# Background products of an attention stage in another order, their weights split half a block ahead, and the heads' loads issued by SP

## The chip, the cores and the metric

The kernel runs on one core of a Trainium2 chip. The metric is the device time of one execution in microseconds (us), taken as the median of several runs. The core's engines each work through a list of instructions of their own, in a fixed order: TensorE (PE) multiplies matrices and writes to the banks of PSUM, VectorE (DVE) and ScalarE (ACT) work element by element, GpSimd (POOL) helps, and SyncE (SP) only issues transfers (DMAs). They wait for each other by semaphores.

## The reference

One decoder layer for a sequence of 512 positions of 1024 channels, in fp32, one layer deep:

```python
x = x + 0.5 * swiglu(rms_norm(x, ffn1_norm), ffn1_w_gate, ffn1_w_up, ffn1_w_down)
h = rms_norm(x, mix_norm)
z = h @ w_in      # its columns: c_q | c_kv | k_rope | dq | dk | dv | gate_mla | gate_diff
y_mla  = mla_branch(c_q, c_kv, k_rope, ...)      # 8 heads, low-rank q and kv, causal
y_diff = diff_branch(dq, dk, dv, ...)            # 4 heads, softmax1 - lambda * softmax2, causal
merged = (sigmoid(gate_mla) * (y_mla @ w_proj_mla)
          + sigmoid(gate_diff) * (y_diff @ w_proj_diff))
x = x + merged @ w_out
x = x + 0.5 * swiglu(rms_norm(x, ffn2_norm), ffn2_w_gate, ffn2_w_up, ffn2_w_down)
return rms_norm(x, final_norm)
```

## The kernel before

Activations lie transposed, channels on the 128 partitions and the 512 positions along the rows. Every fp32 operand is split into a high part rounded to fp32r (names that end in h or hi) and the rest (l or lo), and a product is three matmuls in a row: high weights times low, and so on (`mm3`, lines 116 to 119). A block of weights comes by a DMA on SP's queue into one of two halves of the buffer `raw` (`load`, line 102). `split` (lines 109 and 110) lets ACT cast it to `whi` and DVE subtract that from it to give `wlo`; for seven of the blocks it is POOL that subtracts.

This case is about the middle of the program, the two attention branches. Their own matmuls are short and each step has to pass through a softmax on DVE and ACT, so other matmuls are put between the steps. These are the products of the normed input with the columns of `w_in` for the gates and for dq and dk of the second branch. A product of 128 columns has eight steps (k = 0 to 7) of three matmuls each. The products are written as Python generators, chained into `stream`; `fill(n)` advances it by n steps, and it is called after each attention step as often as `MLA_FILL` and `DIFF_FILL` say. At its first step a product loads its weights, splits them, and multiplies.

- `make_gates(nm, n2)`: two products from one load of 256 columns. Behind each, DVE scales the bank (line 822, `gate`), ACT takes the tanh, and the result is stored to DRAM (`gm_d` or `gd_d`).
- `diff_qk(h)`: the products dq and dk of head h. Behind each, the rotary work: ACT copies the bank to `zr`, SP sends four small DMAs that swap rows (`sw`, lines 843 and 844), DVE makes `z` in three instructions (lines 846 to 848), ACT casts it (`zh`), DVE subtracts (`zl`), and the parts are stored to `qad`, `kad` and `kld` in DRAM.
- The first branch (MLA) takes eight heads of four steps: scores (`bank_sc<-kth,...`), softmax, transposes (`bank_tp<-ident,e`, `ptl`), values (`bank_pv`). Six jobs run beside it, and what is left of them runs behind it.
- The second branch (diff) takes four heads. `diff_load(h)` brings a head from DRAM: `qa`, `ka`, `kl` in two halves, and `dv`, on ACT's queue. A step of `diff_scores` makes two scores of up to 512 columns (lines 992 and 993), each followed by softmax_block: DVE adds the mask and takes the extremum (line 807), ACT takes the exponential (line 809). Then DVE combines both (lines 999 to 1001), PE transposes (line 1009), ACT and DVE split the result into `pt0` and `pt1` (lines 1010 and 1011), and a step later PE multiplies with `dv` (line 1019), and DVE adds the halves (line 1023).

PSUM banks go by tags: three for scores (`sc`), two for the background products (`gb`), two for transposes (`tp`), one for values (`pv`). A fourth score waits until the exponential of the first has read its bank.

The order on each engine in this part isn't that of the code alone: the framework's scheduler decides it when the program is built. On the chip it is then fixed.

Of the kernel before, what the change touches and what calls it, by code (L numbers as in the profile page):

```python
# [15 lines left out]
P = 128  # L16
# [3 lines left out]
KT = DM // P  # L20
# [36 lines left out]
def hybrid_layer_kernel(ctx: ExitStack, tc: tile.TileContext, x, positions,  # L57
# [6 lines left out]
    nc = tc.nc  # L64
# [34 lines left out]
    def load(view, eng=None):  # L99
        _, a, b = view.shape  # L100
        t = space(a, b)
        (eng or nc.sync).dma_start(out=t, in_=view)
        return t
# [708 lines left out]

    def make_gates(nm, n2):
        raw = load(kview(w_in, off[nm] + n2 * 256, off[nm] + (n2 + 1) * 256))
        for s in range(2):
            yield
            ps = bank()

            eng = pool if nm == "gm" and (n2 or s) else vec
            yield from gemm_steps(ps, split(raw[:, :, s * P:(s + 1) * P], eng), kcols, xg)  # L820
            g = zp.tile([P, T], F32, name="gate", tag="z")
            vec.tensor_tensor(out=g, in0=ps, in1=Rb, op=ALU.mult)
            act.activation(g, g, AF.Tanh, scale=0.5)
            nc.sync.dma_start(out=gd_[nm][n2 * 2 + s], in_=g)

# [7 lines left out]
    def diff_qk(h):  # L833
        for j, nm in enumerate(("dq", "dk")):
            yield
            raw = load(kview(w_in, off[nm] + h * P, off[nm] + (h + 1) * P))
            ps = bank()
            yield from gemm_steps(ps, split(raw), kcols, xg)
# [23 lines left out]
        spilled.add(h)  # L862


    jobs = [diff_qk(0), make_gates("gm", 0), diff_qk(1), make_gates("gm", 1), make_gates("gm", 2), make_gates("gm", 3)]
    stream = (u for job in jobs for u in job)
# [98 lines left out]
    jobs = [diff_qk(2), make_gates("gd", 0), diff_qk(3), make_gates("gd", 1), make_gates("gd", 2), make_gates("gd", 3)]  # L965
    stream = (u for job in jobs for u in job)
    heads = {}

    def diff_load(h):
# [7 lines left out]
        act.dma_start(out=as_f32(qa), in_=qad[h].rearrange("(s a) r t -> (a r) s t", s=2))  # L977
        act.dma_start(out=as_f32(ka), in_=kad[h].rearrange("(s a) r t -> (a r) s t", s=2))
        for s in range(2):
            rs = slice(64 * s, 64 * s + 64)  # L980
            act.dma_start(out=as_f32(kl[rs, s, :]), in_=kld[h, rs, :])
        act.dma_start(out=as_f32(dv), in_=dvd[:, h].rearrange("p b u c -> p b (u c)"))
# [66 lines left out]
    diff_load(0)  # L1049
    steps = [(h, i) for h in range(DH) for i in range(NB)]  # L1050
# [248 lines left out]
```

## Time and profile before

| What | us |
|---|---|
| median of 3 runs | 1076.73 |
| lowest, highest run | 1076.37, 1077.65 |
| the profiled execution's own time | 1076.4 |
| its span, first to last instruction | 1074.7 |
| first branch, from its first score | about 430 to 523 |
| second branch, until its last transposes | about 523 to 632 |

The profile is of one execution. Its busy times are of each engine; matmuls are pipelined, so that one begins before the one ahead has ended, and so are DVE's instructions. The granted clock of TensorE was 0.999 of full over the span.

### The profile page before, as it was taken

Reading aid. Unit: us, or ns where it says so; the run is one execution under the profiler, and the core shown is the slowest. Engines: PE = TensorE matmul, PEld = TensorE weight load, DVE = VectorE, ACT = ScalarE, POOL = GpSimd, SP = SyncE. Lnnn points to the kernel's source line nnn. Section 1 sums busy time; section 2 is a strip of 40 time slices with the busy share of each in tenths; the row PEclk is TensorE's granted clock in tenths of the full one; section 3 lists DMA queues with packets and bytes.
Section 4 is the critical chain, followed back from the end, with each engine's and each line's share of the span. In section 5 each row is a group of like instructions: output and inputs, shape, how many; then the busy total and the mean of one; then the engine's idle time right before and its main releaser. Section 6 shows DMA issues by size and latency. Waiting matters only on the chain.

```text
span 1074.7 us, 15826 instructions
## 1 busy us (share of the span) xinstructions
PE 1058.4 (98%) x6272; PEld 934.5 (87%) x6272; DVE 811.7 (76%) x1336; ACT 513.3 (48%) x832; POOL 47.4 (4%) x57
## 2 busy tenths in 40 slices
PE   8999999999999999999999999999999999999997
PEld 6798989999898888788788888888989999898995
DVE  5998797978766767998488868558977767767753
ACT  6462534435254434676356634344525435252544
POOL 1000000000000100012100000000000000000003
PEclk9999999999999999999999999999999999999999
DMA  8314262434215415352767468321242503224211
GB/s 249 126 37 148 79 203 92 114 103 173 83 59 162 124 50 156 92 162 71 225 188 232 121 216 287 114 79 42 79 153 80 158 32 131 74 84 153 79 60 78
DMA packets 106297, 132.90 MB, mean 124 GB/s; under 512 B 4230, under 2 KB 86320, under 8 KB 106224
## 3 DMA queue, kind: packets, MB, share of 16 engines
q1 hardware_dynamic: 96448, 110.80, 32.3%
q10 hardware_dynamic: 7728, 15.18, 4.5%
q0 software_dynamic: 2048, 5.92, 2.0%
q8 instruction: 49, 0.80, 0.3%
q14 instruction: 24, 0.20, 0.1%
HBM read 114.32 MB, written 17.04 MB: 122 GB/s over the span
## 4 chain that ended last, share of the span: by engine, by line
PE 89%; DVE 5%; DMA 3%; ACT 1%; issue 1%; SPq 0%; DVEq 0%; ACTq 0%
PE bank_gb L117 8%; PE bank_gb L119 8%; PE bank_gb L118 8%; PE bank_sc L404 4%; PE bank_sc L402 4%; PE bank_sc L403 4%; PE bank_gb L402 3%; PE bank_gb L404 3%; PE bank_gb L403 3%; PE bank_tp L404 3%; PE bank_tp L403 3%; PE bank_tp L402 3%; PE bank_sc L118 3%; PE bank_sc L119 3%; PE bank_sc L117 2%; PE bank_tp L118 2%
## 5 line engine op out<-in xcount | busy, mean ns | idle before, releaser
L109 ACT CAST whi<-raw 128x1024 fp32r<-128x1024 f32 (+1 forms) x124 | 123.2, 995 | 122.6 <-PE bank_gb L119 31.2
L110 DVE TENSOR_TENSOR wlo<-raw,whi 128x1024 fp32r<-128x1024 f32 (+1 forms) x117 | 134.6, 1150 | 49.2 <-ACT whi L109 49.0
L110 DVE TENSOR_TENSOR wlo<-fraw,whi 128x1024 fp32r<-128x1024 f32 x77 | 92.1, 1196 | 43.5 <-ACT whi L109 43.5
L109 ACT CAST whi<-fraw 128x1024 fp32r<-128x1024 f32 x77 | 79.1, 1027 | 78.0 <-PE bank_gb L119 27.2
L117 PE MATMUL bank_gb<-xh,wlo 128*128 128x512 f32 x256 | 103.2, 403 | 0.5 <-DVE wlo L110 0.5
L119 PE MATMUL bank_gb<-xl,whi 128*128 128x512 f32 x256 | 100.5, 393 | 0.0
L118 PE MATMUL bank_gb<-xh,whi 128*128 128x512 f32 x256 | 100.2, 392 | 0.0
L109 ACT CAST whi<-s 128x1024 fp32r<-128x1024 f32 x36 | 37.8, 1049 | 81.4 <-PE bank_sc L119 15.2
L404 PE MATMUL bank_sc<-xl,whi 128*128 128x256 f32 x224 | 63.5, 283 | 0.0
L403 PE MATMUL bank_sc<-xh,whi 128*128 128x256 f32 x224 | 63.5, 283 | 0.0
L402 PE MATMUL bank_sc<-xh,wlo 128*128 128x256 f32 x224 | 63.5, 283 | 0.0
L119 PEld LDWEIGHTS bank_gb<-xl,whi 128*128 128x128 f32 x256 | 48.1, 188 | 10.2
L117 PEld LDWEIGHTS bank_gb<-xh,wlo 128*128 128x128 f32 x256 | 48.2, 188 | 9.1 <-DVE wlo L110 0.9
L110 DVE TENSOR_TENSOR wlo<-s,whi 128x1024 fp32r<-128x1024 f32 x36 | 44.0, 1222 | 15.8 <-ACT whi L109 15.2
L118 PEld LDWEIGHTS bank_gb<-xh,whi 128*128 128x128 f32 x256 | 48.3, 189 | 8.1
L402 PEld LDWEIGHTS bank_sc<-xh,wlo 128*128 128x128 f32 x224 | 43.0, 192 | 0.1
L403 PEld LDWEIGHTS bank_sc<-xh,whi 128*128 128x128 f32 x224 | 43.0, 192 | 0.1
L404 PEld LDWEIGHTS bank_sc<-xl,whi 128*128 128x128 f32 x224 | 43.0, 192 | 0.0
L404 PE MATMUL bank_tp<-xl,whi 128*128 128x256 f32 x144 | 40.8, 283 | 0.0
L403 PE MATMUL bank_gb<-xh,whi 128*128 128x256 f32 x144 | 40.8, 283 | 0.0
L404 PE MATMUL bank_gb<-xl,whi 128*128 128x256 f32 x144 | 40.8, 283 | 0.0
L403 PE MATMUL bank_tp<-xh,whi 128*128 128x256 f32 x144 | 40.8, 283 | 0.0
(582 smaller groups left out, 3245.8 us busy)
## 6 DMA issues: line engine op xcount, KB each, us to landing
fraw<-in_ffn_w_gate_dram SPq DMA_DIRECT2D x11, 1024.0 KB
fraw<-in_ffn_w_up_dram SPq DMA_DIRECT2D x11, 1024.0 KB
raw<-in_w_in_dram SPq DMA_DIRECT2D x11, 1024.0 KB
raw<-in_ffn_w_gate_dram SPq DMA_DIRECT2D x10, 1024.0 KB
raw<-in_ffn_w_up_dram SPq DMA_DIRECT2D x10, 1024.0 KB
fraw<-in_ffn_w_down_dram SPq DMA_DIRECT2D x4, 2048.0 KB
raw<-in_ffn_w_down_dram SPq DMA_DIRECT2D x4, 2048.0 KB
raw<-in_w_in_dram SPq DMA_DIRECT2D x8, 512.0 KB
```

The source lines that it names most:

```text
L109: act.copy(hi, src)
L110: (eng or vec).tensor_tensor(out=lo, in0=src, in1=as_f32(hi), op=ALU.subtract)
L117: pe.matmul(ps, wl, xh, start=start, stop=False)
L118: pe.matmul(ps, wh, xh, start=False, stop=False)
L119: pe.matmul(ps, wh, xl, start=False, stop=stop)
L402: pe.matmul(o, wl[:, g, k, :], th[:, k, :], start=first and n, stop=False, skip_group_check=True)
L403: pe.matmul(o, wh[:, g, k, :], th[:, k, :], start=False, stop=False, skip_group_check=True)
L404: pe.matmul(o, wh[:, g, k, :], tl[:, k, :], start=False, stop=last, skip_group_check=True)
```

## The change

The generators are taken apart into pairs of functions: `parts` loads and splits a product's weights, `product` multiplies and finishes. A new generator `units` runs them: after the fifth of a product's eight steps (k == KT // 2) it calls `parts` of the next product, so that load and split stand in the program three steps ahead of their first use. The order of jobs beside the first branch was diff_qk(0), gm 0, diff_qk(1), gm 1, gm 2, gm 3, and becomes gm 0, diff_qk(0), gm 1, gm 2, diff_qk(1), gm 3. Beside the second branch it was diff_qk(2), gd 0, diff_qk(3), gd 1, gd 2, gd 3, and becomes diff_qk(2), diff_qk(3), gd 0, gd 1, gd 2, gd 3. Eight steps (`fill(KT)`) run between the load of the first head and its first score. The five DMAs of `diff_load` move from ACT's queue to SP's.

```diff
         return e
 
 
+
     def make_gates(nm, n2):
-        raw = load(kview(w_in, off[nm] + n2 * 256, off[nm] + (n2 + 1) * 256))
-        for s in range(2):
-            yield
+        raw = []
+
+        def parts(s):
+            if s == 0:
+                raw.append(load(kview(w_in, off[nm] + n2 * 256, off[nm] + (n2 + 1) * 256)))
+
+            eng = pool if nm == "gm" and (n2 or s) else vec
+            return split(raw[0][:, :, s * P:(s + 1) * P], eng)
+
+        def product(s, w):
             ps = bank()
-
-            eng = pool if nm == "gm" and (n2 or s) else vec
-            yield from gemm_steps(ps, split(raw[:, :, s * P:(s + 1) * P], eng), kcols, xg)
+            yield from gemm_steps(ps, w, kcols, xg)
             g = zp.tile([P, T], F32, name="gate", tag="z")
             vec.tensor_tensor(out=g, in0=ps, in1=Rb, op=ALU.mult)
             act.activation(g, g, AF.Tanh, scale=0.5)
             nc.sync.dma_start(out=gd_[nm][n2 * 2 + s], in_=g)
 
+        return [(partial(parts, s), partial(product, s)) for s in range(2)]
+
 
     sws = [zp.tile([P, T], F32, name=f"sw{j}", bufs=1) for j in range(2)]
     for t in sws:
...
     spilled = set()
 
     def diff_qk(h):
-        for j, nm in enumerate(("dq", "dk")):
-            yield
-            raw = load(kview(w_in, off[nm] + h * P, off[nm] + (h + 1) * P))
+        def parts(nm):
+            return split(load(kview(w_in, off[nm] + h * P, off[nm] + (h + 1) * P)))
+
+        def product(nm, j, w):
             ps = bank()
-            yield from gemm_steps(ps, split(raw), kcols, xg)
+            yield from gemm_steps(ps, w, kcols, xg)
             zr = zp.tile([P, T], F32, name="zr", bufs=1)
             act.copy(zr, ps)
             sw = sws[j]
...
                 for u in range(4):
                     nc.sync.dma_start(out=kad[h, u], in_=hi[u // 2])
                 nc.sync.dma_start(out=kld[h], in_=as_f32(zl))
-        spilled.add(h)
-
-
-    jobs = [diff_qk(0), make_gates("gm", 0), diff_qk(1), make_gates("gm", 1), make_gates("gm", 2), make_gates("gm", 3)]
-    stream = (u for job in jobs for u in job)
+            if j:
+                spilled.add(h)
+
+        return [(partial(parts, nm), partial(product, nm, j)) for j, nm in enumerate(("dq", "dk"))]
+
+    def units(jobs, w=None):
+        us = [u for job in jobs for u in job]
+        w = w or us[0][0]()
+        for n, (_, product) in enumerate(us):
+            yield
+            for k, _ in enumerate(product(w)):
+                if k == KT // 2 and n + 1 < len(us):
+                    w = us[n + 1][0]()
+                yield
+
+
+    jobs = [make_gates("gm", 0), diff_qk(0), make_gates("gm", 1), make_gates("gm", 2), diff_qk(1), make_gates("gm", 3)]
+    stream = units(jobs)
 
     def fill(n=1):
         for _ in range(n):
...
     for t in kls:
         for s in range(2):
             pool.memset(as_f32(t[64 - 64 * s:128 - 64 * s, s, :]), 0.0)
-    jobs = [diff_qk(2), make_gates("gd", 0), diff_qk(3), make_gates("gd", 1), make_gates("gd", 2), make_gates("gd", 3)]
-    stream = (u for job in jobs for u in job)
+    jobs = [diff_qk(2), diff_qk(3), make_gates("gd", 0), make_gates("gd", 1), make_gates("gd", 2), make_gates("gd", 3)]
+    stream = units(jobs, jobs[0][0][0]())
     heads = {}
 
     def diff_load(h):
...
         ka = df.tile([P, 2, T], F32R, name="ka")
         kl = kls[h % 2]
         dv = df.tile([P, NB, 2 * P], F32R, name="dv")
-        act.dma_start(out=as_f32(qa), in_=qad[h].rearrange("(s a) r t -> (a r) s t", s=2))
-        act.dma_start(out=as_f32(ka), in_=kad[h].rearrange("(s a) r t -> (a r) s t", s=2))
+        nc.sync.dma_start(out=as_f32(qa), in_=qad[h].rearrange("(s a) r t -> (a r) s t", s=2))
+        nc.sync.dma_start(out=as_f32(ka), in_=kad[h].rearrange("(s a) r t -> (a r) s t", s=2))
         for s in range(2):
             rs = slice(64 * s, 64 * s + 64)
-            act.dma_start(out=as_f32(kl[rs, s, :]), in_=kld[h, rs, :])
-        act.dma_start(out=as_f32(dv), in_=dvd[:, h].rearrange("p b u c -> p b (u c)"))
+            nc.sync.dma_start(out=as_f32(kl[rs, s, :]), in_=kld[h, rs, :])
+        nc.sync.dma_start(out=as_f32(dv), in_=dvd[:, h].rearrange("p b u c -> p b (u c)"))
         heads[h] = qa, ka, kl, dv, df.tile([P, NB, P], F32, name="o4"), small.tile([P, 8, NB], F32, name="hst", bufs=2)
 
     def diff_scores(h, i):
...
         yd.append((yh, yl))
 
     diff_load(0)
+    fill(KT)
     steps = [(h, i) for h in range(DH) for i in range(NB)]
     pend = {}
     for k in range(len(steps) + 7):
```

The rows that follow are the orders on the engines as the program is built; a name's number tells which buffer it is. First PE in the second branch, before, where head 1 ends and head 2 begins: L1019 multiplies with `dv`, L992 and L993 are a score, L117 to L119 are steps of a background product.

```order
L1019 MATMUL bank_pv_5780<-dv_5309,pt0_5668 128x256
L1019 MATMUL bank_pv_5780<-dv_5309,pt1_5669 128x256
L992 MATMUL bank_sc_5789<-ka_5564,qa_5563 128x128
L993 MATMUL bank_sc_5789<-kl0_5261,qa_5563 128x128
L117 MATMUL bank_gb_5737<-xh1_3237,wlo_5739 128x512
L118 MATMUL bank_gb_5737<-xh1_3237,whi_5738 128x512
L119 MATMUL bank_gb_5737<-xl1_3238,whi_5738 128x512
L117 MATMUL bank_gb_5818<-xh0_3235,wlo_5820 128x512
L118 MATMUL bank_gb_5818<-xh0_3235,whi_5819 128x512
L119 MATMUL bank_gb_5818<-xl0_3236,whi_5819 128x512
```

A score of head 2 is followed by six matmuls of background products. The same place with the change, L1042 being the values, L1015 and L1016 a score:

```order
L1042 MATMUL bank_pv_5833<-dv_5356,pt0_5735 128x256
L1042 MATMUL bank_pv_5833<-dv_5356,pt1_5736 128x256
L1015 MATMUL bank_sc_5842<-ka_5627,qa_5626 128x128
L1016 MATMUL bank_sc_5842<-kl0_5261,qa_5626 128x128
L1015 MATMUL bank_sc_5859<-ka_5627,qa_5626 128x128
L1016 MATMUL bank_sc_5859<-kl0_5261,qa_5626 128x128
L1015 MATMUL bank_sc_5904<-ka_5627,qa_5626 128x256
L1016 MATMUL bank_sc_5904<-kl0_5261,qa_5626 128x256
L1042 MATMUL bank_pv_5883<-dv_5356,pt0_5825 128x256
L1042 MATMUL bank_pv_5883<-dv_5356,pt1_5826 128x256
```

Three scores of head 2 now follow each other with nothing of the background between, then values. After two more scores (bank_sc_5924, bank_sc_5975) and a transposition come 48 matmuls of gd 1 in one piece. A like run stands one head earlier (scores from bank_sc_5480 to bank_sc_5712), ahead of 48 matmuls of dk of head 3 and of gd 0.

DVE at the second of these runs, with the change (L808 is the mask with the extremum and its read-out, L1024 the combination, L111 the split):

```order
L808 ISA bank_sc_5859,hst_5635<-bank_sc_5859,cmask_3521 128x128
L808 ISA hst_5635 128x1
L1046 TENSOR_TENSOR o4_5362<-bank_pv_5883,o4_5362 128x128
L808 ISA bank_sc_5904,hst_5635<-bank_sc_5904,cmask_3521 128x256
L808 ISA hst_5635 128x1
L1022 RECIPROCAL hst_5635<-hst_5635 128x1
L808 ISA bank_sc_5924,hst_5635<-bank_sc_5924,cmask_3521 128x256
L808 ISA hst_5635 128x1
L1023 TENSOR_SCALAR hst_5635<-hst_5635,nlam_3913 128x1
L808 ISA bank_sc_5975,hst_5635<-bank_sc_5975,cmask_3521 128x384
L808 ISA hst_5635 128x1
L111 TENSOR_TENSOR wlo_5723<-raw_75,whi_5722 128x1024
```

The last row is the low part of the weights with which the 48 matmuls begin (`wlo_5723`); it stands behind the mask of the run's last score.

SP with the change, ahead of the weights of dk of head 3 (the first `raw` row) and of gd 0 (the second):

```order
L1004 DMA kl1_5262<-kld_3547 64x512
L866 DMA qad_3545<-zh_5328 64x512 x2
L867 DMA qad_3545<-zl_5329 128x512
L1004 DMA kl1_5262<-kld_3547 64x512
L1005 DMA dv_5356<-dvd_3550 128x1024
L853 DMA sw1_4119<-zr_5396 8x512
L854 DMA sw1_4119<-zr_5396 8x512
L853 DMA sw1_4119<-zr_5396 8x512
L854 DMA sw1_4119<-zr_5396 8x512
L103 DMA raw_75<-in_w_in_dram 128x8x128
L103 DMA raw_75<-in_w_in_dram 128x8x256
```

Head 1's loads stand between the stores of head 2's q (`qad`) and the four swaps of its k, and the two loads of weights behind them. Before, SP had only the stores, the swaps and the weights.

## Rows read from the trace of the kernel before

**Rows 1.** The page: the span, and part 1 (busy time and share).

```profile
span 1074.7 us, 15826 instructions
...
PE 1058.4 (98%) x6272; PEld 934.5 (87%) x6272; DVE 811.7 (76%) x1336; ACT 513.3 (48%) x832; POOL 47.4 (4%) x57
```

**Rows 2.** Busy time of each engine in the two attention stretches.

```profile
430.00:523.00 93.00, 91.39 (x482) 76.84 (x481) 82.97 (x213) 60.95 (x143) 16.79 (x7) 1.00 0.39 111
523.00:632.00 109.00, 106.97 (x550) 89.31 (x549) 85.25 (x276) 60.10 (x168) 2.09 (x4) 1.00 0.63 191
```

**Rows 3.** Waits of PE in both stretches: total us, times, longest.

```profile
PE bank_sc L993 <- DMA kl<-kld: 0.9, 1, 0.9
PE bank_sc L992 <- ACT e L809: 0.8, 2, 0.7
PE bank_pv L925 <- DVE ptl L912: 0.6, 2, 0.3
PE bank_gb L117 <- DVE wlo L110: 0.5, 1, 0.5
```

**Rows 4.** Timeline of PE at 445 us: start, length, line, names, idle before.

```profile
444.30 0.28 PE L925 MATMUL bank_pv<-ptl,vt 128*128 128x256 f32 x1
444.42 0.22 PE L924 MATMUL bank_pv<-pth,vt 128*128 128x128 f32 x1
444.47 0.28 PE L925 MATMUL bank_pv<-ptl,vt 128*128 128x128 f32 x1
445.29 0.50 PE L117 MATMUL bank_gb<-xh,wlo 128*128 128x512 f32 x1 [0.54 <-DVE wlo L110]
```

**Rows 5.** Timeline of PE and ACT at 546 us.

```profile
546.09 0.71 ACT L809 ACTIVATE e<-bank_sc,hst 128x512 f32<-128x512 f32 x1
...
546.94 0.33 PE L992 MATMUL bank_sc<-ka,qa 128*128 128x128 f32 x1 [0.67 <-ACT e L809]
...
547.51 0.39 PE L118 MATMUL bank_gb<-xh,whi 128*128 128x512 f32 x1
...
547.74 0.40 PE L119 MATMUL bank_gb<-xl,whi 128*128 128x512 f32 x1
```

**Rows 6.** Timeline of DVE at 446 us.

```profile
446.10 0.67 DVE L846 TENSOR_TENSOR z<-bank_gb,table 128x512 f32<-128x512 f32 x1
446.70 0.68 DVE L807 CUSTOM_DVE_ANT_0 bank_sc<-bank_sc,cmask 128x512 f32<-128x512 f32 x1
```

**Rows 7.** DVE by line and shape, 536 to 632 us (busy, mean ns | idle before).

```profile
L110 DVE TENSOR_TENSOR wlo<-raw,whi 128x1024 fp32r<-128x1024 f32 x10 | 12.2, 1218 | 1.6 <-ACT whi L109 1.6
L807 DVE CUSTOM_DVE_ANT_0 bank_sc<-bank_sc,cmask 128x512 f32<-128x512 f32 x8 | 5.6, 697 | 1.0 <-PE bank_sc L993 1.0
L822 DVE TENSOR_TENSOR gate<-bank_gb,Rb 128x512 f32<-128x512 f32 x8 | 5.5, 686 | 1.0 <-PE bank_gb L119 1.0
L1023 DVE TENSOR_TENSOR o<-bank_pv,o 128x128 f32<-128x128 f32 x16 | 4.5, 284 | 0.4 <-ACT o L1022 0.4
L807 DVE CUSTOM_DVE_ANT_0 bank_sc<-bank_sc,cmask 128x384 f32<-128x384 f32 x8 | 4.5, 563 | 4.8 <-PE bank_sc L993 4.8
L1000 DVE TENSOR_SCALAR hst<-hst,nlam 128x1 f32<-128x1 f32 x16 | 4.3, 270 | 0.2
...
L807 DVE CUSTOM_DVE_ANT_0 bank_sc<-bank_sc,cmask 128x256 f32<-128x256 f32 x7 | 2.9, 434 | 1.6 <-PE bank_sc L993 1.1 <-ACT e L809 0.5
...
L999 DVE RECIPROCAL hst<-hst 128x1 f32<-128x1 f32 x16 | 2.5, 159 | 1.8 <-ACT e L809 1.6
```

**Rows 8.** Timelines of SP and ACT: a weight load's issue, its landing.

```profile
556.50 0.38 SPq L102 DMA_DIRECT2D raw<-in_w_in_dram  x1
...
564.68 1.05 ACT L109 CAST whi<-raw 128x1024 fp32r<-128x1024 f32 x1 [2.30 <-DMA raw<-in_w_in_dram]
```

**Rows 9.** Timelines of POOL and DVE at 483 us.

```profile
483.18 2.40 POOL L110 TENSOR_TENSOR wlo<-raw,whi 128x1024 fp32r<-128x1024 f32 x1 [7.47 <-ACT whi L109]
...
483.72 2.41 DVE L933 TENSOR_TENSOR yml<-yf,ymh 128x512 fp32r<-128x512 f32 x1
```

More of the change, by code (lines that the diff above doesn't have):

```diff
@@ L1 @@
 import math
+from functools import partial
 from contextlib import ExitStack
```

## The prediction

> **What bounds the kernel now.** I read the page first, to see which engine has no slack. TensorE is busy for 1058.4 of 1074.7 us [rows 1], so nothing but its pauses can be won, and anything that makes it pause is lost. The table by stretch comes next: the change touches the two attention branches alone, and there TensorE is idle for 1.61 of 93 us and for 2.03 of 109 us, 3.64 together, while DVE is busy for 82.97 and 85.25 [rows 2]. The reader is to see two things there: little can be won, and DVE, which feeds both the softmax and the weight splits, is at 89% and 78% of its time, near enough to full that the order of its work matters.
>
> The waits of TensorE say what the idle time is for [rows 3]: 0.9 us for a head's `kl`, 0.8 in two waits for an exponential that frees a score bank, 0.6 in two for `ptl`, 0.5 for a split. They come to 2.8 us in six waits. A wait costs more than its idle time, because matmuls overlap: one of 512 columns lasts 0.39 us, and the next starts 0.23 after it [rows 5], so each break also takes about 0.16. From start to start the break at 445 us is 0.82 (444.47 to 445.29), where an undisturbed step is some 0.1 [rows 4]. So the six waits are worth 2.8 + 6 x 0.16 = 3.8 us. The other 0.84 of the 3.64 lies in shorter breaks.
>
> **The change part by part.** *What no sum needs.* TensorE gets the same matmuls, POOL the same seven splits, ACT loses twenty issues of transfers. Only order and waits count.
>
> *First branch.* In the new order a gate product stands first, and the two rotary pairs are farther apart. On DVE the work per head becomes more even, and a split stands three steps (nine matmuls, 9 x 0.23 = 2.1 us) ahead of its first use. The waits for `wlo` and `ptl` (1.1 us in three, 1.6 with their breaks) should go, the first wait of the softmax should stay.
>
> *Second branch, what goes.* Eight steps, 24 matmuls or 24 x 0.23 = 5.5 us, come between the load of the first head and its score, and cover the 0.9 us for `kl`. The two score waits at 546 us stand at a place that is filled otherwise now. Together 1.7 us in three, 2.2 with breaks.
>
> From both branches that is 3.8. I add the shorter breaks, 0.84, since most stand at rotary work or at transposes that move too, and get 4.6 given back. The bounds: 3.0, if a third of it comes back elsewhere, and 5.9, if the whole 3.64 goes with some fourteen breaks (14 x 0.16 = 2.2).
>
> *Second branch, what comes.* This is the heart of it. With both rotary pairs first, the fills of `DIFF_FILL` no longer spread over all heads as they did. The scheduler leaves two runs of scores, transposes and values with no product between them, and each ends before 48 matmuls that need a split. In DVE's list that split stands behind all the softmax work of the run (the rows of the order shown above). So TensorE has only the run's own matmuls to do, while DVE has to get through all that stands ahead of the split, and DVE's part is longer.
>
> The second run, as the example. I count from the transposes just ahead of its first score, for DVE can't begin the first instruction of its list (the `pt1` of those transposes) before them. From there to the split DVE has 22 instructions, besides the short read-outs, which start together with the next: seven of 512 columns (two masks, `sw`, `z`, `zl`, the gate, one combination) at about 0.69, two of 384 at 0.56, three of 256 at 0.43, five of 128 at 0.284, two `hst` at 0.27, two reciprocals at 0.16, and the split at 1.22 [rows 7]. Instructions that aren't masks are put at the row of the same width. That is 4.83 + 1.13 + 1.30 + 1.42 + 0.54 + 0.32 + 1.22 = 10.76. An instruction starts some 0.08 before the last has ended (446.10 + 0.67 against 446.70 [rows 6]); 21 x 0.08 = 1.7, so 9.1 us. To this come 0.6 until DVE can begin (the tail of the transposes and ACT's pass over 256 columns, about half of the 0.71 in [rows 5]) and 0.1 until TensorE starts again: 9.8. TensorE has meanwhile 7 matmuls of 512 columns at 0.23, 2 of 384 at 0.18 (between the two neighbours), 16 of 256 and 11 of 128 at 0.12 [rows 4, 5]: 1.61 + 0.36 + 1.92 + 1.32 = 5.2. It stands for 4.6 us.
>
> The first run in the same way: seven of 512, one of 384, two of 256, five of 128, two `hst`, four reciprocals and the like, the split: 4.83 + 0.56 + 0.87 + 1.42 + 0.54 + 0.64 + 1.22 = 10.08, less 1.7, and 0.7 at the ends: 9.1. TensorE has 7, 4, 24 and 11: 1.61 + 0.72 + 2.88 + 1.32 = 6.5. It stands for 2.6 us.
>
> Both are floors, because they let DVE run without a gap. In the trace it stands for 1.6 us ahead of seven masks of 256 columns (0.2 each) and for 4.8 ahead of eight of 384 (0.6 each) [rows 7]. I take one hand-over of 0.3 a run, between these two: 2.9 + 4.9 = 7.8. The bounds: 7.2 with none, 8.4 with 0.6 each.
>
> *The loads on SP.* The five of a head stand ahead of the weights of the next products. A weight load of 1 MB issued at 556.50 was waited for by ACT until 564.68, 8.2 us [rows 8]; the loads of the products in question are issued with some 1 to 2.6 us more than that in hand. I put them at 0. With the cover gone, each us of lateness is one us of wait at the same split: 2 to 3 us at most for the bytes of one head ahead of it.
>
> The sum: 1076.4 (the profiled execution's own time, 0.3 below the median shown) - 4.6 + 7.8 = 1079.6 us.
>
> **The rivals.**
>
> *(a) Faster: the runs are cheap.* The nearest wait that the trace shows where scores follow each other is 0.67 us, 0.83 with its break [rows 5]. Were the runs to cost this each, the sum would be 1076.4 - 4.6 + 1.7 = 1073.5. The point that decides: DVE has to have finished the split within TensorE's 5.2 and 6.5 us. For it speaks that the kernel has had only short waits at such places; against it, that the split then stood beside products that TensorE could do meanwhile.
>
> *(b) No change: floors and the whole give-back.* DVE's runs at 7.2 and 5.9 given back: 1076.4 + 1.3 = 1077.7, and up to 0.7 less if breaks too short for the idle time to show go as well. For it: each count above is of one list and its order is fixed; against it: every short break has to vanish.
>
> *(c) Slower still: transfers.* The head's loads and the weights share the way, and the weights land 2 to 3 us after the cover: 1079.6 + 2.5 = 1082.1. For it speak the 8.2 us of [rows 8], against it that SP issues long before. The Trainium skill, page "DMA: Bandwidth & Descriptors", section "Issuing engines are not separate DMA queues", says that transfers started by different engines run on the same 16 DMA engines and interleave, and that a second issuer saves only the issuing. By that rule the move from ACT to SP would win nothing at the transfers themselves. No row here shows the two issuers beside each other.
>
> *(d) Slower still: POOL beside DVE.* A split on POOL that took from 483.18 for 2.40 us had beside it a subtraction on DVE of 2.41 us that is otherwise some 0.69 [rows 9, 7]. In the first branch POOL's splits meet other DVE work now; one more such meeting on the path costs 2.41 - 0.69 = 1.7: 1081.3. Against it: there are as many such splits as before. The Trainium skill, page "SBUF — State Buffer", section "Who interferes with whom", says that a DVE instruction with two inputs in SBUF contends with a GpSimd instruction that reads SBUF, and that one fully blocks while the other has the shared ports. The row agrees, with 2.41 us.
>
> **How the numbers follow.** Some 0.2% (2.15 us, so 1074.6 and 1078.9) is what a measurement of this kernel can tell from no change. The forecast has 0.42, with 1078.9 to 1080.9 as its own range (give-back 5.3 to 3.9 against 7.8, or the runs at their ends); (b) 0.28, since its terms are only the bounds of mine; (c) 0.14; (d) 0.08; (a) 0.08. Slower: 0.42 + 0.14 + 0.08 = 0.64. No change: 0.28 and a trace of (a), 0.29. Faster: the rest, 0.07. The range reaches down to the end of (b), 1077.0, and up through (d) and most of (c), to 1082.6; (a) and the edges are left out.
>
> **What would show it.** Right: in the changed profile TensorE has two waits for `wlo` on DVE in the second branch, of about 3 and 5 us, each right ahead of 48 matmuls, and DVE is busy without a gap before them; the first branch is idle for under 0.7 us. Wrong: several short waits for score banks in place of two long ones (then DVE isn't late at the split but at the masks, and the sum may stay), a split that waits for ACT's cast and that for `raw` (rival c), or first-branch waits of the old size (the evenness was no gain). The prediction fails in size if DVE has done part of the list before the transposes from which I count.

## The result

The changed kernel takes 1083.18 us (median of 6 runs, 1082.35 to 1085.68), the kernel before, run beside it, 1077.14 (6 runs). The ratio is 1.0065, with a 95% interval of 1.0052 to 1.0078: slower by 5.6 to 8.4 us. The forecast was 1079.6 with a range to 1082.6. The side was right; of the change, 7.0 us by the ratio, the forecast had 3.2 (1079.6 against the 1076.4 from which it counts).

The profiled execution took 1084.88 us (span 1083.2), 8.5 more than that of before. The line of its page that answers to [rows 1]:

```profile
PE 1063.3 (98%) x6272; PEld 937.4 (87%) x6272; DVE 812.4 (75%) x1336; ACT 513.3 (47%) x832; POOL 47.6 (4%) x57
```
TensorE's share of busy time is the same 98%, but its busy time has grown by 4.9 us with the same 6272 matmuls. A matmul that lasts longer counts as busy, so the share hides part of a loss. The table by stretch shows where (as [rows 2]; the column behind POOL's is the granted clock of TensorE, as a share of full speed):

```profile
430.00:523.00 93.00, 92.72 (x491) 78.53 (x491) 82.69 (x214) 61.96 (x144) 14.41 (x6) 1.00 0.37 105
549.00:558.00 9.00, 7.10 (x42) 5.29 (x41) 8.72 (x27) 7.23 (x23) 0.00 (x0) 1.00 0.68 205
577.00:584.00 7.00, 4.31 (x18) 3.15 (x18) 6.06 (x23) 6.42 (x20) 0.00 (x0) 0.70 1.01 338
580.00:584.00 4.00, 2.49 (x9) 1.78 (x8) 3.06 (x13) 3.93 (x12) 0.00 (x0) 0.50 0.94 306
584.00:590.50 6.50, 6.20 (x15) 4.87 (x16) 3.24 (x9) 1.33 (x5) 0.00 (x0) 0.53 1.02 294
```
The first branch gained: TensorE is idle for 0.28 us of its 93 where it was for 1.61. The loss lies in the second branch, most of it at the two runs that the forecast named (here around 549 to 558 and 577 to 584 us) and behind the second of them. There the clock is at 0.53, and it had fallen to 0.50 inside the run already, from 580 us on. The largest waits of TensorE from 430 to 585 us (as [rows 3]: total, times, longest) are:

```profile
PE bank_sc L1015 <- ACT e L810: 2.4, 4, 1.2
PE bank_gb L118 <- DVE wlo L111: 1.8, 1, 1.8
PE bank_sc L1015 <- DMA ka<-kad: 1.7, 1, 1.7
PE bank_pv L1042 <- DVE pt L1034: 0.5, 1, 0.5
PE bank_pv L1042 <- ACT pt L1033: 0.3, 1, 0.3
```
The waits for `kl` and the split of the first branch are gone from this list, and in the place of the first stands one for `ka`, twice as long. The rest are the two runs, and only one of these waits is for a split. The first run, on TensorE's timeline, from its first values to the 48 matmuls behind it:

```profile
547.22 0.48 PE L1042 MATMUL bank_pv<-dv,pt 128*128 128x256 f32 x2
...
551.11 0.39 PE L1015 MATMUL bank_sc<-ka,qa 128*128 128x256 f32 x1 [0.59 <-ACT e L810]
...
554.25 0.38 PE L1042 MATMUL bank_pv<-dv,pt 128*128 128x256 f32 x1 [0.34 <-ACT pt L1033]
555.00 0.44 PE L1015 MATMUL bank_sc<-ka,qa 128*128 128x384 f32 x1 [0.37 <-ACT e L810]
...
556.17 1.09 PE L1042 MATMUL bank_pv<-dv,pt 128*128 128x256 f32 x7 [0.55 <-DVE pt L1034]
557.30 0.50 PE L118 MATMUL bank_gb<-xh,wlo 128*128 128x512 f32 x1
```
It lasts from 547.22 to 557.30, 10.1 us, for what the forecast counted as 6.5 us of TensorE's work: 3.6 more, where 2.9 was forecast. TensorE is idle in four breaks of 0.34 to 0.59 us for ACT and DVE, 1.85 together and 2.5 with the 0.16 a break; the other 1.1 are steps of its own that were put too short (six values of 256 columns start 0.135 apart, 551.59 to 552.40, where 0.12 was put down). It doesn't wait for `wlo` here: DVE is through with the split (556.03 and 1.22) at the moment at which TensorE is through with its last values.

```profile
547.91 0.42 DVE L1034 TENSOR_TENSOR pt<-bank_tp,pt 128x256 fp32r<-128x256 f32 x1
...
556.03 1.22 DVE L111 TENSOR_TENSOR wlo<-raw,whi 128x1024 fp32r<-128x1024 f32 x1
```
DVE's list for this run takes 9.3 us, where 8.4 and 0.3 were put down. The second run on TensorE:

```profile
573.37 0.48 PE L1042 MATMUL bank_pv<-dv,pt 128*128 128x256 f32 x2
...
577.62 0.33 PE L1015 MATMUL bank_sc<-ka,qa 128*128 128x128 f32 x1 [1.17 <-ACT e L810]
...
580.22 0.58 PE L1015 MATMUL bank_sc<-ka,qa 128*128 128x256 f32 x1
...
581.99 0.52 PE L1016 MATMUL bank_sc<-kl,qa 128*128 128x384 f32 x1
584.30 0.79 PE L118 MATMUL bank_gb<-xh,wlo 128*128 128x512 f32 x1 [1.79 <-DVE wlo L111]
584.89 0.63 PE L119 MATMUL bank_gb<-xh,whi 128*128 128x512 f32 x1
585.32 0.63 PE L120 MATMUL bank_gb<-xl,whi 128*128 128x512 f32 x1
...
590.28 0.39 PE L120 MATMUL bank_gb<-xl,whi 128*128 128x512 f32 x1
```
From its first values (573.37) to 584.30 it lasts 10.9 us for 5.2 of work: 5.7 more, where 4.9 was forecast. Of this TensorE is idle for 3.5 (1.17, 0.23, 0.33 and 1.79). Part of the rest is the clock: the eight matmuls from 580.22 to the end of the score at 582.51 take 2.3 us, and the same eight in the first run, at full clock, 1.5 (552.40 to 553.91). Behind the run the step from matmul to matmul of 512 columns is 0.43 us (584.89 to 585.32), and 0.23 again from 590.28 on. There are 14 steps from 584.30 to 590.28: 5.98 us in place of 14 x 0.23 = 3.2, so 2.8 us more are lost after the wait has ended. DVE's list in the same run:

```profile
574.05 0.42 DVE L1034 TENSOR_TENSOR pt<-bank_tp,pt 128x256 fp32r<-128x256 f32 x1 [2.75 <-ACT pt L1033]
...
582.54 0.57 DVE L808 CUSTOM_DVE_ANT_0 bank_sc<-bank_sc,cmask 128x384 f32<-128x384 f32 x1 [0.79 <-PE bank_sc L1016]
...
583.03 2.35 DVE L111 TENSOR_TENSOR wlo<-raw,whi 128x1024 fp32r<-128x1024 f32 x2
```
DVE begins at 574.05, 0.6 after the transposes, as forecast. It stands still for only 0.15 and 0.79 us until the split, and the second of these is the score that TensorE was late with at half clock. It needs 10.2 us from 574.05 to the end of the first split (583.03 and 1.22), where 9.1 and 0.3 were put down: the 0.8 that is missing is that wait.

The wait for the first head, on SP's queue and on TensorE:

```profile
522.16 2.41 SPq L870 DMA_DIRECT2D kad<-zh  x4
...
526.28 0.84 SPq L1001 DMA_DIRECT2D ka<-kad  x1
```

```profile
532.36 0.39 PE L118 MATMUL bank_gb<-xh,wlo 128*128 128x512 f32 x1
534.46 0.30 PE L1015 MATMUL bank_sc<-ka,qa 128*128 128x128 f32 x1 [1.72 <-DMA ka<-kad]
```
The stores of head 1's k are issued from 522.16 on, and the load of head 0's k soon behind them, at 526.28. TensorE has work until 532.74 and then stands for the load until 534.46: 8.2 us after its issue, in spite of the eight steps.

### The profile page after: what moved, and what is told of

Its sections match the earlier page's. It is cut to its first block, busy times and chain, and to the rows that moved or that the text cites. A ratio compares the mean times of both kernels' runs of the same rounds, so it can differ in the third digit from the quotient of the medians.

```text
span 1083.2 us, 15840 instructions
## 1 busy us (share of the span) xinstructions
PE 1063.3 (98%) x6272; PEld 937.4 (87%) x6272; DVE 812.4 (75%) x1336; ACT 513.3 (47%) x832; POOL 47.6 (4%) x57
## 4 chain that ended last, share of the span: by engine, by line
PE 90%; DVE 4%; DMA 3%; ACT 1%; SPq 1%; issue 1%; DVEq 0%; ACTq 0%
PE bank_gb L118 8%; PE bank_gb L119 8%; PE bank_gb L120 8%; PE bank_sc L405 4%; PE bank_sc L403 4%; PE bank_sc L404 4%; PE bank_gb L403 3%; PE bank_gb L405 3%; PE bank_gb L404 3%; PE bank_tp L405 3%; PE bank_tp L404 3%; PE bank_tp L403 3%; PE bank_sc L119 3%; PE bank_sc L118 3%; PE bank_sc L120 3%; PE bank_tp L119 2%
## 5 line engine op out<-in xcount | busy, mean ns | idle before, releaser
L111 DVE TENSOR_TENSOR wlo<-raw,whi 128x1024 fp32r<-128x1024 f32 (+1 forms) x117 | 134.5, 1151 | 48.2 <-ACT whi L110 47.9
L111 DVE TENSOR_TENSOR wlo<-fraw,whi 128x1024 fp32r<-128x1024 f32 x77 | 92.2, 1197 | 43.5 <-ACT whi L110 43.5
L119 PE MATMUL bank_gb<-xh,whi 128*128 128x512 f32 x256 | 101.1, 395 | 0.0
L119 PEld LDWEIGHTS bank_gb<-xh,whi 128*128 128x128 f32 x256 | 49.0, 192 | 8.5
L111 DVE TENSOR_TENSOR wlo<-s,whi 128x1024 fp32r<-128x1024 f32 x36 | 44.1, 1224 | 15.2 <-ACT whi L110 14.4
```

The costliest lines, as they stand in the source:

```text
L111: (eng or vec).tensor_tensor(out=lo, in0=src, in1=as_f32(hi), op=ALU.subtract)
L119: pe.matmul(ps, wh, xh, start=False, stop=False)
```

## The experiments

Each ratio is to the kernel before on the same chip; "us by ratio" is (ratio - 1) x 1077. By that measure the change itself is +7.0 (5.6 to 8.4).

| Kernel | median us | ratio (95%) | us by ratio |
|---|---|---|---|
| loads on ACT | 1079.17 | 1.0014 (1.0003 to 1.0025) | +1.5 |
| second order undone | 1075.32 | 0.9980 (0.9968 to 0.9992) | -2.2 |
| no eight steps | 1079.86 | 1.0034 (1.0019 to 1.0049) | +3.7 |
| no split ahead | 1084.81 | 1.0069 (1.0052 to 1.0086) | +7.4 |
| both orders undone | 1074.02 | 0.9972 (0.9961 to 0.9983) | -3.0 |
| second order undone, loads on ACT | 1084.84 | 1.0072 (1.0060 to 1.0084) | +7.8 |
| twenty matmuls more | 1083.77 | 1.0068 (1.0053 to 1.0082) | +7.3 |
| second order undone, early second pair | 1073.04 | 0.9962 (0.9949 to 0.9975) | -4.1 |
| second order undone, twelve steps | 1075.64 | 0.9993 (0.9982 to 1.0005) | -0.8 |
| old orders, no split ahead | 1074.25 | 0.9981 (0.9971 to 0.9991) | -2.0 |
| kernel before, second order alone | 1084.08 | 1.0069 (1.0056 to 1.0083) | +7.4 |
| old orders, no eight steps | 1078.59 | 1.0013 (1.0001 to 1.0026) | +1.4 |
| old orders, loads on ACT | 1079.60 | 1.0020 (1.0003 to 1.0036) | +2.2 |

### One part undone at a time

**Loads on ACT.** All five issues of `diff_load` as here:

```diff
-        nc.sync.dma_start(out=as_f32(qa), in_=qad[h].rearrange("(s a) r t -> (a r) s t", s=2))
+        act.dma_start(out=as_f32(qa), in_=qad[h].rearrange("(s a) r t -> (a r) s t", s=2))
```

> The changed kernel with one part undone: the five loads of a head are issued by ACT again. In the program's order the two runs of scores without a product are gone with it. Theory 1 (the time is lost in the two runs, where a split stands late on DVE, and in the half clock behind the second): the waits of TensorE at the runs, 2.8 and 5.2 us, and the half-clock matmuls after them, 2.6 us, go, so about 10 us less than the changed kernel's 1083: 1072 to 1075. Rival theory 2 (the loads themselves land late on SP's queue, nothing else): only the 1.7 us wait for a head's ka goes, about 1081. Rival theory 3 (the split half a block ahead puts it behind the softmax): no change, 1083.

It came out 5.5 us below the changed kernel, half of what theory 1 said and more than theory 2. The two runs are gone from the trace, but a wait for `kl` of 1.2 us is there (533.70), and a new one in head 0's last step. ACT's timeline there, and TensorE's:

```profile
542.88 0.59 ACT L850 COPY zr<-bank_gb 128x512 f32<-128x512 f32 x1 [1.52 <-DMA sw<-zr]
...
543.36 0.27 ACT L1033 CAST pt<-bank_tp 128x128 fp32r<-128x128 f32 x1
```

```profile
543.68 0.38 PE L1042 MATMUL bank_pv<-dv,pt 128*128 128x256 f32 x1 [1.46 <-ACT pt L1033]
```
ACT stands for 1.52 us at the copy to `zr`, since that single buffer is still being read by the swaps; the `pt` that TensorE needs is behind the copy in ACT's list. Matmuls of 0.63 us, at half clock, follow here too. This isn't the new second order's doing: the copy is the second of head 2's own pair, and with the second order old and the loads on ACT it waits nearly as long (1.35 us, below).

**The second order undone.**

```diff
-    jobs = [diff_qk(2), diff_qk(3), make_gates("gd", 0), make_gates("gd", 1), make_gates("gd", 2), make_gates("gd", 3)]
+    jobs = [diff_qk(2), make_gates("gd", 0), diff_qk(3), make_gates("gd", 1), make_gates("gd", 2), make_gates("gd", 3)]
```

> The changed kernel with one part undone: the order of jobs beside the second branch is that of before (rotary, gate, rotary, gates); loads stay on SP, eight steps and the split ahead stay. The runs are gone in the program's order. Theory 1: waits at the runs and the half clock go, the wait of 1.7 us for ka stays: 1073 to 1076. Theory 2 (late loads on SP): nothing of it moves, about 1082 to 1083. Theory 3 (split ahead): about 1083.

As theory 1 said: from +7.0 to -2.2, so the second order costs 9 us in these surroundings. The loads are still on SP and the split is still ahead, so theories 2 and 3 fall. The longest wait that is left to TensorE is one of 2.2 us for the first head's `ka`.

**No eight steps.**

```diff
     diff_load(0)
-    fill(KT)
```

> The changed kernel with one part undone: no eight steps between the load of the first head and its first score. The runs are gone in the program's order too. Theory 1: as in the last, 1073 to 1076, unless the loads of two heads, which now stand behind each other ahead of the next weights, bring a wait of their own of 1 to 3 us. Theory 2: the first score waits longer for its head, 1083 to 1086. Theory 3: about 1083.

The long runs are gone, and 3.3 us with them, but theory 1's 1073 to 1076 is missed. One long wait stands in their place:

```profile
PE bank_gb L118 <- DVE z L856: 3.5, 1, 3.5
```
A product can't start because DVE hasn't read the bank of the product two ahead of it (`z`, the rotary work); behind it 14 matmuls run at half clock. The bank is that of head 3's k, the last of the four rotary products in a row. Without the eight steps and with both orders old (below, +1.4) this wait is gone and the time is 2.3 us shorter.

**No split ahead** (`parts` is called at a product's own first step):

```diff
             yield
+            if not ahead:
+                w = us[n][0]()
             for k, _ in enumerate(product(w)):
-                if k == KT // 2 and n + 1 < len(us):
+                if ahead and k == KT // 2 and n + 1 < len(us):
                     w = us[n + 1][0]()
```

> The changed kernel with one part undone: a product loads and splits its weights at its own first step, in both branches, as before. The two runs stay in the program's order (5.0 and 3.7 us of TensorE's own work without a product). Theory 1: about 1083, within 2 us, with both long waits still in the trace. Theory 3 (the split ahead is the cause): about 1075. If the split ahead hid something in the first branch, waits for wlo there come back, at most 2 us.

Theory 1's number, and theory 3 falls. Both runs are in its trace, with waits of the same size (1.8 us for `wlo` in the second). Its profiled execution was 2.6 us shorter than that of the changed kernel (spans 1080.6 and 1083.2), and its table shows why:

```profile
577.00:584.00 7.00, 4.33 (x18) 3.36 (x18) 6.06 (x23) 6.23 (x20) 0.00 (x0) 0.76 1.02 343
584.00:590.50 6.50, 6.28 (x27) 5.18 (x28) 3.62 (x10) 1.43 (x6) 0.00 (x0) 1.00 0.95 274
```
Here too the clock falls inside the run (0.64 from 580 to 584 us), but it is back at 1.00 from 584 us on. As far as the means tell, how long half clock lasts differs between executions of the same kernel: the mean granted clock of this one's six runs is 0.994 to 0.998, that of the changed kernel's six 0.994 to 0.996, where the profile of before has 0.999. By these means the clock fell in each run of the changed kernel, but the 2.8 us are the figure of one execution, not a fixed term.

### The hole and the clock

**Twenty matmuls more.** In the product behind the second run:

```diff
             ps = bank()
+            if (nm, n2, s) == ("gd", 1, 0):
+                for _ in range(20):
+                    pe.matmul(ps, xg[0][0][:, 0:P], xg[0][0], start=True, stop=True)
             yield from gemm_steps(ps, w, kcols, xg)
```

> The changed kernel with 20 matmuls of 512 columns more (20 x 0.23 = 4.5 us of TensorE's work whose result is thrown away) in the bank of the product behind the second run; they stand ahead of the run. Theory 1 (TensorE stands there for DVE, 5.2 us, and goes to half clock for standing): the added work fills the hole, the half-clock matmuls behind it are gone, and the time is not longer than the changed kernel's 1083 by the 4.5 us, but between 1080 and 1084. If TensorE's work there were what counts (no hole, or a clock that falls for another reason): 1087 to 1088.

4.5 us of work were added, and the ratio went from 1.0065 to 1.0068: the work was done while TensorE would have stood, as theory 1 said. Its table for the stretches of the second run:

```profile
577.00:584.00 7.00, 4.85 (x28) 3.91 (x27) 5.67 (x15) 3.79 (x9) 0.00 (x0) 1.00 0.96 322
584.00:590.50 6.50, 6.50 (x34) 5.47 (x33) 1.48 (x4) 2.03 (x8) 0.00 (x0) 1.00 0.89 252
```

```profile
590.00 0.96 PE L1045 MATMUL bank_pv<-dv,pt 128*128 128x256 f32 x6
```
The clock is 1.00 throughout in this execution, the shortest of the kernel's six. The test isn't a clean one: with the added matmuls the scheduler ordered the run anew. Its last four transposes and six values, which in the changed kernel stand ahead of the split, come behind the 48 matmuls here (590.00), and a wait of 1.7 us for `wlo` is left. That added work shortens the standing is shown; that the order alone would not have done it isn't.

### The orders, apart from each other

**Both orders undone** (the two lines of `jobs` as before, the rest as changed).

> The changed kernel with both orders of jobs as before; the split ahead, the eight steps and the loads on SP stay. Beside the kernel with only the second order undone (1075.3) it tells what the first order is worth. Theory A (the first order evens out DVE's work and is worth the 2.5 us of waits that went from the first branch, and the wait for ka comes from the stores of dk of head 1, which that order puts right ahead of the head's loads): the waits of the first branch come back, up to 2.5 us, the wait for ka falls from 2.4 us to under 1.2: 1075 to 1078. Theory B (the split ahead alone took the waits from the first branch, and ka waits because SP issues it): first branch as with the new order, ka as late as before: 1075, no change.

0.8 us faster than with the second order alone undone, with intervals that overlap: the first order wins nothing that could be measured. The 1074.02 us lie below theory A's 1075 to 1078.

```profile
430.00:523.00 93.00, 91.26 (x481) 76.54 (x480) 83.10 (x213) 61.07 (x143) 16.84 (x7) 1.00 0.38 110
523.00:590.00 67.00, 67.00 (x343) 56.67 (x342) 52.05 (x144) 38.17 (x98) 2.09 (x4) 1.00 0.79 239
```
The waits of the first branch are back (1.74 us idle), as theory A said, and the second branch is without any idle time until 590 us: the wait for `ka` is gone altogether. But the load of head 0 comes no earlier: it is issued at 527.24, and TensorE begins the first score at 534.97, later than the 534.46 of the changed kernel. So what the first order gives in one branch the other loses, since TensorE comes to the first score 2.2 us earlier and the load doesn't. That the stores ahead of the load make it late, theory A's second half, isn't shown by this. Theory B falls with the waits of the first branch, which the split ahead doesn't take away.

**The rotary pair of head 1 one place earlier.**

```diff
-    jobs = [make_gates("gm", 0), diff_qk(0), make_gates("gm", 1), make_gates("gm", 2), diff_qk(1), make_gates("gm", 3)]
+    jobs = [make_gates("gm", 0), diff_qk(0), make_gates("gm", 1), diff_qk(1), make_gates("gm", 2), make_gates("gm", 3)]
```

> The changed kernel with the second order undone, and in the first the rotary pair of head 1 one place earlier (gate, rotary, gate, rotary, gate, gate), so that its stores don't stand right ahead of the first head's loads. Theory A (stores and loads crowd each other at 522 to 535 us): the wait for ka or kl falls from 2.4 us to under 1.2, and if the first branch keeps its waits away, 1073 to 1074.5. Theory 2 (SP's queue itself): the wait stays, 1075.

1073.04 us, the fastest here: 0.25 to 0.51% below the kernel before, and below the changed one. The wait for the head is 0.2 us. The first branch didn't keep its waits away (`ptl`, 1.4 in two), and that alone can account for the head's wait being gone:

```profile
526.67 0.52 SPq L1001 DMA_DIRECT2D ka<-kad  x1
```

```profile
534.38 0.22 PE L1015 MATMUL bank_sc<-ka,qa 128*128 128x128 f32 x1
```
The load is issued 0.4 us later than in the changed kernel, and TensorE, idle for 2.0 us of the first branch, begins the first score at 534.38, when the changed kernel's wait had 0.1 us to go. The load need have landed only 0.1 us sooner. With the stores right ahead of it the score could begin 7.0 to 8.7 us after the load's issue (7.0 with twenty matmuls more, 7.6 without the split ahead, 8.2, 8.7 with the second order undone); without them it was there within 7.7 in both kernels. So crowding of stores and loads is not shown, and neither is SP's queue: theory A gave the number, for another reason.

**Twelve steps ahead** (`fill(KT + 4)`, second order undone).

> The changed kernel with the second order undone (1075.3) and twelve steps in place of eight ahead of the first score: 4 x 3 x 0.23 = 2.7 us more cover for the first head. Theory A (the transfers end at about 535 us whatever stands ahead of the score, and half clock follows the wait): the wait for ka, 2.4 us, and the half-clock matmuls behind it, 1.7 us, go: 1071 to 1073. Rival: the four steps are missing later and a wait as long comes up at another place: 1075.

The rival was right. The wait for the head is gone, and others have come up behind it: 1.9 us in two for exponentials (L810) and 1.2 for `wlo`.

**The second order alone**, in the kernel before.

> The kernel before with the new order of jobs beside the second branch alone (rotary, rotary, gates): no split ahead, no eight steps, loads on ACT. No run of scores without a product stands in its order. Theory 1, in its narrow form (only the long runs cost): about as before, 1075 to 1079. Its wide form (two rotary pairs in a row hold up ACT and DVE in any case, since both share one buffer for the copy and four swaps each): waits of 2 to 5 us come up beside head 1: 1079 to 1083.

It costs all of the change's loss, though its program has no long run. That is a little more than the wide form of theory 1 said, and by a mechanism that neither form had named. ACT's and TensorE's timelines of this kernel:

```profile
565.92 0.38 ACTq L978 DMA_DIRECT2D ka<-kad  x1
```

```profile
568.12 0.39 PE L993 MATMUL bank_sc<-kl,qa 128*128 128x512 f32 x1
574.12 0.44 PE L992 MATMUL bank_sc<-ka,qa 128*128 128x128 f32 x1 [5.62 <-DMA ka<-kad]
...
574.83 0.73 PE L117 MATMUL bank_gb<-xh,wlo 128*128 128x512 f32 x1
```
and of the kernel before:

```profile
566.03 0.38 ACTq L978 DMA_DIRECT2D ka<-kad  x1
```

```profile
575.23 0.30 PE L992 MATMUL bank_sc<-ka,qa 128*128 128x128 f32 x1 [0.17 <-DMA sw<-zr]
```
The load of head 2's k is issued at the same moment in both. Before, TensorE has products to do until 575.23; with the new order it has nothing more ahead of the score from 568.12 on and stands for 5.6 us. Before, the products in this time are those of head 3's q and k (ACT copies their banks at 570.46 and 577.96). With the new order these are done earlier, and TensorE's list has the score next and the next product only behind it (574.83). Why the scheduler put it there is not shown.

### The other three parts without the new orders

**Old orders, no split ahead.**

> Both orders as before and no split ahead, so that of the change only the eight steps and the loads on SP are left. Beside the one with both orders undone (1074.0) it tells what the split ahead is worth: by the trace of that one the second branch has hardly an idle moment, so if it is the split that did it, waits for wlo come back and it is 1075 to 1077; if the eight steps and SP did it, 1074, no change.

No difference from both orders undone that could be measured (-2.0 against -3.0, intervals overlap): the split ahead is worth nothing here.

**Old orders, no eight steps.**

> Both orders as before and no eight steps; the split ahead and the loads on SP stay. Beside the one with both orders undone (1074.0) it tells what the eight steps are worth: the wait of about 1 us for a head ought to come back, 1075 to 1076; if the loads on SP alone took it away, 1074.

Dearer by 4.4 us than with them, more than expected. Waits for `ka` of 2.4 us in two are back, with matmuls at half clock behind the first.

**Second order undone, loads on ACT; old orders, loads on ACT** (the edit to `diff_load` shown first, added to those).

> The changed kernel with the second order undone and the loads back on ACT. Beside the one with only the order undone (1075.3): if SP's queue delays the heads (theory 2), the wait of 2.4 us for a head goes and it is 1073 to 1074. If the transfers themselves are what is slow (theory A), the wait stays within 0.8 us of 2.4, and ACT is held up by its issues: 1075 to 1078.

Both theories missed it: 10 us dearer than on SP. It is also 6.3 us dearer than the kernel with the loads on ACT and the second order new (+7.8 against +1.5): with the loads on ACT the new second order is the faster one. TensorE's longest waits are now on ACT and DVE, and one is the wait behind the copy to `zr` that the first run of this section showed:

```profile
PE bank_pv L1042 <- DVE o L1046: 2.0, 1, 2.0
...
PE bank_pv L1042 <- ACT pt L1033: 1.4, 1, 1.4
```

```profile
544.85 0.59 ACT L850 COPY zr<-bank_gb 128x512 f32<-128x512 f32 x1 [1.35 <-DMA sw<-zr]
```
That left open whether the loss needs the new first order.

> Both orders as before and the loads on ACT; of the change only the split ahead and the eight steps are left. Beside the one with the loads on SP (1074.0) it tells what the move of the loads is worth where no order is changed. If the loads stand in ACT's list behind its softmax work and come late for that (what the run on ACT with the first order new showed, 1084.8), 1079 to 1085. If that loss needs the new first order, 1074 to 1077.

With both orders as before ACT costs 5.2 us against SP (+2.2 and -3.0), in the lower part of the first expectation. The longest wait is for ACT's exponential, with half clock behind it:

```profile
PE bank_sc L1015 <- ACT e L810: 2.2, 1, 2.2
```

```profile
543.08 0.62 ACT L861 CAST zh<-z 128x512 fp32r<-128x512 f32 x1 [2.77 <-DVE z L858]
```
The exponential stands right behind this cast in ACT's list, and the cast waits for the rotary work. So the move to SP saves 5 to 10 us where the second order isn't new, and in the changed kernel going back to ACT saves 5.5. In these three kernels ACT stands for the rotary swaps or for the work behind them (1.52, 1.35 and 2.77 us) with something behind it that TensorE needs. Whether the loads in its list bring that about was not tried by itself and stays open.

## Why the forecast was right in its side and wrong in its size

**The runs.** The core of the mechanism was right: each run lasts as long as DVE's list up to the split, DVE is busy all but without a gap (8.72 of 9 us in the first), and the floors of 2.6 and 4.6 us aren't undercut. The form of the waits was not. The sign named for being right, two waits for `wlo` of about 3 and 5 us, didn't appear: there is one, of 1.8 us, and of the 5.4 us that TensorE is idle in the runs 2.4 are for exponentials that free a score bank, which the forecast had listed as a sign of being wrong, with the note that the sum may stay. The sum was 3.6 + 5.7 = 9.3 us in place of 7.8, beyond the bound of 8.4. Two terms were too small: DVE's list in the first run, 9.3 us in place of 8.4 and 0.3 for the hand-over, and the hand-over in the second, where DVE waits 0.8 us for the score that half clock delays.

**The first head, the step that failed.** "Eight steps [...] cover the 0.9 us for `kl`", and the loads on SP "I put them at 0". TensorE stands for 1.72 us (1.9 with its break) for `ka` in place of being 1.1 better off. I had compared the cover with a weight load's 8.2 us of [rows 8] for the weights alone, and not with the head's own load: issued at 526.28, awaited until 534.46. And I had given back the first branch's waits as if nothing stood behind them: TensorE comes to the first score earlier by what it no longer waits there, and the load doesn't. The two kernels in which the first branch keeps its waits have none, or 0.2 us, at the head. Whether the stores of head 1 ahead of the load, rival (c)'s crowding at another load, make it late stays open: those two kernels don't settle it. The page "DMA: Bandwidth & Descriptors" of the Trainium skill, section "Issuing engines are not separate DMA queues", says that transfers run on the same engines whoever issues them. The two kernels with both orders new don't speak against it: issued by ACT, the last awaited part of the first head was there at 533.70, by SP at 534.46. The same section grants another issuer only the time that its sequencer needs to start the transfer, and calls it usually small. For the time of this kernel the choice isn't small, as ACT and SP differ by 5 us with both orders old; no run tells whether that is the issuing itself.

**The clock, a term that was missing.** Every wait was priced by its length alone. From 580 us on, inside the second run, TensorE ran at half clock, 1.2 in place of 2.4 GHz. In the profiled execution this cost the 0.8 us above and 2.8 behind the run. No row of before showed it, since its clock was at 0.999.

With these three, each against what the forecast had in its place (7.8, nothing and nothing), the sum is 1079.6 + 1.5 + 1.9 + 2.8 = 1085.8, against the profiled 1084.88. The 0.9 between them is not accounted for. The forecast's own range was also put too wide at its upper end: 1080.9 needs the smaller give-back and the longer runs at once, and either alone gives 1080.3 or 1080.2.

**The first branch** gave back as forecast: idle time fell from 1.61 to 0.28 us, 1.3 before the breaks, where 1.1 were put down for its three waits. But the evenness brought nothing in the end, since the time won was spent waiting for the head.

**What the forecast had not seen** is that the price of the second order hangs on the other parts, and doesn't need the two runs. I tied it to these runs in one program's order. Beside the other parts of the change it costs 9.2 us (+7.0 against -2.2). Alone in the kernel before, where the runs don't exist, it costs 7.4, through a score whose head isn't there yet. Without the eight steps both orders together cost 2.3 (+3.7 against +1.4), through a bank. And with the loads on ACT it costs nothing: new, it is at +1.5, old, at +7.8 or, with the first order old as well, at +2.2. So 9 us are not the price of the order as such. The other three parts, with the old orders, make the kernel faster by 3.0 us. Rival (a) was refuted by the runs' size, (b) by the same. Rival (c), as it was put, isn't in the trace: the split of the second run follows the mask at once (583.03) and waits for no weights. Of (d) nothing was seen: the first branch lost none of its gain.

## What to carry to other kernels

Work that fills the gaps of a latency-bound stage is also the cover for its next loads; before it is put in another order, ask for each load what TensorE will be doing until it lands. Price a wait with what comes after it, here the half clock, and a stage that is made faster with the load for which the next stage will then stand. Of a change with five parts, time the parts, and in more than one surrounding: here three were good for 3 us and one cost 9 beside them, but that one cost nothing with the loads on ACT.

## What the runs showed of the hardware

In the second run of the changed kernel TensorE was idle for 1.17, 0.23 and 0.33 us one after the other, with little work between. Then its granted clock fell to 0.50 of full (580 to 584 us), with no longer idle time before it, and matmuls of 512 columns behind the run followed each other in 0.43 in place of 0.23 us until 590.28. In the profiled execution of the kernel without the split ahead, with idle times equal within 0.01 us, it fell at the same place (0.64 from 580 to 584 us) and was back at 1.00 from 584 us on. In the kernel before with the second order alone 5.6 us of standing were followed by half clock too (matmuls 0.63 us long at 575.36, where 0.39 is the rule).

The load of a head's k, 512 KB, was awaited until 7.0 to 8.7 us after its issue in the four kernels that issue it at about 526 us on SP's queue with the stores of head 1's k ahead of it and wait for it.
